# Diagonal key blocks of 384 and 128 queries in one bank with one exponential, and one product for both halves of the rotated sliding keys

## The chip, the core and the metric

The kernel runs on one NeuronCore of a Trainium2 chip. The metric is the device time of one execution in microseconds (us). Engines are named as in the profile: PE is TensorE, DVE is VectorE, ACT is ScalarE, POOL is GpSimd, SP is SyncE, which here issues nearly all DMAs. Each of them takes its instructions in the order in which they were laid down for it, and they meet at semaphores alone. SBUF is the working memory, PSUM the memory that PE writes.

## The reference, cut to what matters

Two transformer blocks are computed one after the other on 2048 tokens of width 1024. The first block has eight heads of "forgetting" attention (called fox in the code) and eight query heads of a sliding-window attention with two key heads. The second has an attention over keys that an indexer selected (called dsa in the code, eight heads, 16 meta tokens ahead of the keys), and beside it a gated recurrence. The lines that the change bears on are these:

```python
half = HEAD_DIM // 2                        # rope, on qb (8 heads) and kb (2 heads)
x1, x2 = xf[..., :half], xf[..., half:]
return concat([x1 * cos - x2 * sin, x2 * cos + x1 * sin], axis=-1)
...
s = einsum('bhqd,bhkd->bhqk', qb, kh) * scale + cb[..., None] - cum[:, :, None, :]
s = where(key_pos <= q_pos, s, -inf)        # causal
p = softmax(s, axis=-1)
return einsum('bhqk,bhkd->bhqd', p, vh)
```

The second attention has the same form, with a mask of selected keys and a bias by distance added to the scores.

## The kernel before

**Number format.** A product of float32 quality is made of three float16 products: each operand is split into a high and a low part, and high x high, high x low and low x high are summed in PSUM.

**The projections of the first block** stream weight blocks through `load_w` (four loads `wraw`, scaled on DVE in L282, cast on ACT in L283, low part on POOL in L284) and multiply each with the normalised activations. `mm3_T` (L319) makes one transposed product: eight steps over the contraction, three products in each (L326, L327, L328), each of 512 columns. `rotated` (L504) makes the queries and keys of the sliding attention. Rope needs the two halves of each head as two separate tensors, so `rotated` makes two products for each of the four groups of 512 tokens, one for each half, in two PSUM tiles `pp` (the pool has two). For the queries each half has 128 rows (four heads of 32), for the keys, the block `kb`, 64 rows (two heads of 32). Four DVE instructions multiply them with cosine and sine (L523 and L524, into tiles `ra`), POOL adds or subtracts (L525), and `store_rot` splits the result (ACT L480, POOL L481, into one of two tiles `ehi`) and writes it to DRAM (L482, `d_kb` for the keys).

**The attention units.** A unit is one head h and one group g of 512 queries. `main` runs over key blocks of 128 keys, j = 0 to 4g + 3. For the last four blocks, those on the diagonal, only the queries from 128 (j - 4g) on count, so they have 512, 384, 256 and 128 columns. In `block`, PE makes the scores in a PSUM tile `pst` (fox L982, L984, the causal mask L986; dsa L2103, L2104, bias L2111 and L2113, key masks L2115), `Att.weights` takes the exponential on ACT (L746), casts it to its high part `phi` (L748 on ACT, a small share in L750 on DVE), subtracts for the low part `plo` (L752, mostly POOL), and `Att.pv` multiplies both with the values, three products for each 128 queries (L776, L777, L778), summed in the PSUM tile `po`. After the last block `norm` divides by the row sums (in dsa after a copy of `po` on ACT, L2123). There are two `pst` tiles in fox and three in dsa, three of each of `p32`, `phi` and `plo`, and one `po`. Beside a unit's blocks runs the preparation of a later one, whose row maxima are found on DVE (L963 in fox, L2058 in dsa) and turned into rows of the query tile (L763 to L769).

**What sets the order.** The program text gives an order and priorities, and a scheduler lays the instructions of each engine down by them and by its own estimate of when each is ready. The order on each engine is therefore a result of the build and can move everywhere when something is changed at one place. The fox units of heads 0 to 3 lie among the projections of the first block, those of heads 4 to 7 among the sliding units and the output projection, the dsa units among the recurrence and the second output projection.

Of the kernel before, what the change touches and what calls it, by code (L numbers as in the profile page):

```python
# [10 lines left out]
F32 = mybir.dt.float32  # L11
# [456 lines left out]
def blocks1(K, A, h, sp, wp, er, ps, pso, fa, cum):  # L468

    nc = K.nc  # L470
# [33 lines left out]
    def rotated(kind, c0, m):  # L504
        def f(w, inv, rn):
# [10 lines left out]
            for g in range(NG):  # L516
                p = [ps.tile([128, 512], F32, name="pp")[:m] for _ in range(2)]
                for a in range(2):
                    mm3_T(K, p[a], w, a * m, h[g])
# [170 lines left out]
def fox_gates(K, A, sp, pp, fa, cum, tag):  # L690
# [28 lines left out]
    nc.vector.tensor_scalar(K.clim, K.clim, 2.0 ** 14, None, op0=ALU.mult)  # L719

# [187 lines left out]
def phase_first(K, A, sk):  # L908
# [4 lines left out]
    with ExitStack() as st, ExitStack() as sr:  # L913
# [59 lines left out]
        def main(g, h, ops):  # L973
            KA, KB, QA, QB, v = ops
            po = pso.tile([128, 4, 65], F32, name="po")

            def block(j):
                s0 = max(0, j - 4 * g)
                c0 = s0 * 128
                ks = slice(j * 128, (j + 1) * 128)  # L980
                p = pst.tile([128, 512], F32, name="pst")
                nc.tensor.matmul(p[:, c0:], lhsT=KA[:69, ks], rhs=QA[:69, c0:], start=True, stop=False)  # L982
                diag = j >= 4 * g
                nc.tensor.matmul(p[:, c0:], lhsT=KB[:, ks], rhs=QB[:, c0:], start=False, stop=not diag)  # L984
                if diag:
                    nc.tensor.matmul(p[:, s0 * 128:s0 * 128 + 128], lhsT=K.idb, rhs=K.mT, start=False, stop=True)  # L986
                hi, lo = at.weights(p[:, c0:], K.fci[:, h // 4:h // 4 + 1])
                for s in range(s0, 4):
                    c = slice((s - s0) * 128, (s - s0) * 128 + 128)
                    at.pv(po[:, s], hi[:, c], lo[:, c], v[:, j], first=j == 0 and s == 0, last=j == 4 * g + s)  # L990
# [987 lines left out]
def phase_dsa(K, A, out):  # L1978

    nc, tc = K.nc, K.tc  # L1980
    with ExitStack() as st:
# [98 lines left out]
        def main(g, h, ops, mk):  # L2080
# [17 lines left out]
            def block(j):  # L2098
                s0 = max(0, j - 4 * g)
                c0 = s0 * 128  # L2100
                ks = slice(16 + j * 128, 16 + (j + 1) * 128)
                p = pst.tile([128, 512], F32, name="pst")
                nc.tensor.matmul(p[:, c0:], lhsT=KA[:66, ks], rhs=QA[:66, c0:], start=True, stop=False)  # L2103
                nc.tensor.matmul(p[:, c0:], lhsT=KB[:, ks], rhs=QB[:, c0:], start=False, stop=False)  # L2104
                if j >= 4 * g - 1:

                    b0 = max(0, min(256, (j - 4 * g) * 128))
                    d0 = 4 * g * 128 + b0 - j * 128
                    for a in range(2):
                        if d0 < 0:  # L2110
                            nc.tensor.matmul(p[:, 384:], lhsT=jr, rhs=bT[:, a, :128], start=False, stop=False)  # L2111
                        else:
                            nc.tensor.matmul(p[:, b0:b0 + 256], lhsT=jr, rhs=bT[:, a, d0:d0 + 256], start=False, stop=False)  # L2113
                for s in range(s0, 4):
                    nc.tensor.matmul(p[:, s * 128:s * 128 + 128], lhsT=mk[s][:, j * 128:(j + 1) * 128], rhs=K.idb, start=False, stop=s == 3)  # L2115
                hi, lo = at.weights(p[:, c0:], K.dci[:, h // 4:h // 4 + 1])
                for s in range(s0, 4):
                    c = slice((s - s0) * 128, (s - s0) * 128 + 128)
                    at.pv(po[:, s], hi[:, c], lo[:, c], v[:, j + 1], last=j == 4 * g + s)
# [214 lines left out]
```

## Time and profile before

| | |
|---|---|
| median of 3 runs | 3169.38 us (3162.87 to 3175.8) |
| the profiled execution: its own time | 3170.48 us |
| its span, first to last instruction | 3168.7 us |
| PE busy | 2822.7 us, 89% |
| DVE, ACT, POOL busy | 2101.6, 1686.9, 1450.2 us |
| matmuls | 25152 |

The span is 1.8 us shorter than the execution's own time, and the execution is 1.1 us over the median. A busy engine here means that some instruction of it is under way. Matmuls overlap each other in the pipeline, so what a matmul takes from PE is read from the distance between the starts of two that follow each other, not from its mean duration.

### The profile page before, as it was taken

To read this page: it belongs to the slowest core of one execution; us is meant where nothing else is said; L and a number is where in the kernel's file an instruction comes from. 1 tells how busy PE (TensorE), PEld (TensorE's weight loads), DVE (VectorE), ACT (ScalarE), POOL (GpSimd) and SP (SyncE) were. 2 spreads that over 40 slices of the span, in tenths; PEclk is the share of its full clock that TensorE was granted. 3 is DMA by queue.
4 is the path that set the end of the run, shared out by engine and by line. 5 is a ranking of instruction groups with operands and counts; after the bars stand their busy time and mean duration, and the time that the engine had idled before them with its cause. 6 is when DMAs were issued, how large, how long until landed. Compare 5 with 4: busy or idle time off the path is not lost. (4 is left out here: it accounts for less than half of the span.)

```text
span 3168.7 us, 65862 instructions
## 1 busy us (share of the span) xinstructions
PE 2822.7 (89%) x25152; PEld 1858.8 (59%) x25152; DVE 2101.6 (66%) x5073; ACT 1686.9 (53%) x3058; POOL 1450.2 (46%) x1241
## 2 busy tenths in 40 slices
PE   7899999999997899999998889899678888988997
PEld 5554444477884555544445665358566566666663
DVE  7523765566678676646499699830578778888763
ACT  4423665576566655634356466321455456657763
POOL 3211446564333555534233433610456567768752
PEclk9899999999996799999999989899679989999998
DMA  6222343532235343334433532222753444443331
GB/s 235 82 87 84 105 129 111 173 95 69 79 94 167 109 142 108 124 91 157 111 97 101 160 125 73 89 91 63 182 159 102 137 133 113 118 117 110 122 97 59
DMA packets 271184, 364.28 MB, mean 115 GB/s; under 512 B 60205, under 2 KB 192033, under 8 KB 269705
## 3 DMA queue, kind: packets, MB, share of 16 engines
q1 hardware_dynamic: 270424, 359.96, 37.8%
q8 instruction: 199, 3.26, 0.4%
q14 instruction: 129, 1.05, 0.1%
q10 hardware_dynamic: 432, 0.02, 0.0%
HBM read 247.05 MB, written 112.82 MB: 114 GB/s over the span
## 5 line engine op out<-in xcount | busy, mean ns | idle before, releaser
L752 POOL TENSOR_TENSOR plo<-p,phi 128x512 f16<-128x512 f32 (+3 forms) x600 | 664.9, 1121 | 569.9 <-ACT phi L748 360.0
L748 ACT CAST phi<-p 128x512 f16<-128x512 f32 (+3 forms) x649 | 347.0, 554 | 84.2 <-PE po L778 75.1
L746 ACT ACTIVATE p<-pst,shift,dci 128x512 f32<-128x512 f32 (+4 forms) x352 | 247.4, 716 | 137.2 <-POOL plo L752 46.7
L778 PE MATMUL po<-v,plo 128*128 128x65 f16 x2176 | 270.1, 196 | 35.0 <-POOL plo L752 27.9
L776 PE MATMUL po<-v,phi 128*128 128x65 f16 x2176 | 286.4, 197 | 5.3 <-ACT phi L748 4.2
L777 PE MATMUL po<-v,phi 128*128 128x64 f16 x2176 | 285.3, 198 | 0.0
L778 PEld LDWEIGHTS <-plo 128*128 128x128 f16 x2424 | 234.7, 101 | 79.2 <-POOL plo L752 46.8
L746 ACT ACTIVATE p<-pst,shift,fci 128x512 f32<-128x512 f32 (+1 forms) x320 | 220.1, 710 | 113.1 <-PE pst L984 70.2
L963 DVE TENSOR_REDUCE mu<-p 128x1 f32<-128x512 f32 (+2 forms) x320 | 188.4, 603 | 130.1 <-PE p L959 83.3
L776 PEld LDWEIGHTS <-phi 128*128 128x128 f16 x2424 | 236.1, 100 | 48.8 <-ACT phi L748 11.4
L284 POOL TENSOR_TENSOR wlo<-wraw,whi 128x512 f16<-128x512 f32 (+3 forms) x116 | 149.9, 1310 | 216.9 <-ACT whi L283 214.0
L2058 DVE CUSTOM_DVE_ANT_0 jk<-p,mk 128x512 bf16<-128x512 f32 (+2 forms) x320 | 193.4, 604 | 80.5 <-PE p L2052 32.8
L777 PEld LDWEIGHTS <-phi 128*128 128x128 f16 x2424 | 235.6, 100 | 15.3 <-issue 1.8
L337 PE MATMUL pp<-whi,hhi 128*128 128x256 f16 (+2 forms) x824 | 235.0, 286 | 7.7 <-ACT whi L283 5.7
L339 PE MATMUL pp<-whi,hlo 128*128 128x256 f16 (+2 forms) x824 | 233.2, 285 | 4.2 <-POOL hlo L465 4.2
L338 PE MATMUL pp<-wlo,hhi 128*128 128x256 f16 (+2 forms) x824 | 234.7, 285 | 0.6 <-POOL wlo L284 0.6
L326 PE MATMUL pp<-hhi,whi 128*128 128x512 f16 (+2 forms) x496 | 190.7, 384 | 4.4 <-DVE ra L523 4.4
L328 PE MATMUL pp<-hhi,wlo 128*128 128x512 f16 (+2 forms) x496 | 190.3, 384 | 0.0
L327 PE MATMUL pp<-hlo,whi 128*128 128x512 f16 (+2 forms) x496 | 190.0, 383 | 0.0
L328 PEld LDWEIGHTS <-wlo 128*128 128x128 f16 (+2 forms) x1000 | 99.7, 100 | 122.6 <-POOL wlo L284 10.9
L326 PEld LDWEIGHTS <-whi 128*128 128x128 f16 (+2 forms) x1000 | 100.5, 101 | 120.1 <-issue 10.2
L327 PEld LDWEIGHTS <-whi 128*128 128x128 f16 (+2 forms) x1000 | 99.9, 101 | 117.3 <-issue 16.0
(666 smaller groups left out, 8933.6 us busy)
## 6 DMA issues: line engine op xcount, KB each, us to landing
wraw<-in_w_in_dram SPq DMA_DIRECT2D x88, 256.0 KB
d_z<-er SPq DMA_DIRECT2D x128, 128.0 KB
bT<-d_rb SPq DMA_DIRECT2D x32, 384.0 KB
wa<-in_w_ada_dram SPq DMA_DIRECT2D x8, 1024.0 KB
x<-in_x_dram SPq DMA_DIRECT2D x16, 512.0 KB
d_k<-ehi SPq DMA_DIRECT2D x32, 256.0 KB
d_q<-ehi SPq DMA_DIRECT2D x32, 256.0 KB
QA<-d_q SPq DMA_DIRECT2D x64, 128.0 KB
```

What stands on the lines that cost most here:

```text
L326: nc.tensor.matmul(ps, lhsT=whi, rhs=hhi[:, kk, :], start=kk == 0, stop=False)
L327: nc.tensor.matmul(ps, lhsT=whi, rhs=hlo[:, kk, :], start=False, stop=False)
L328: nc.tensor.matmul(ps, lhsT=wlo, rhs=hhi[:, kk, :], start=False, stop=kk == KK - 1)
L337: nc.tensor.matmul(ps, lhsT=hhi[:, kk, s], rhs=whi, start=kk == 0, stop=False)
L338: nc.tensor.matmul(ps, lhsT=hhi[:, kk, s], rhs=wlo, start=False, stop=False)
L339: nc.tensor.matmul(ps, lhsT=hlo[:, kk, s], rhs=whi, start=False, stop=kk == KK - 1)
L746: nc.scalar.activation(p, s, AF.Exp, scale=ci[:m], bias=K.shift[:m])
L748: nc.scalar.copy(hi, p)
L752: e.tensor_tensor(lo, p, hi, op=ALU.subtract)
L776: nc.tensor.matmul(o, lhsT=hi, rhs=v[:, :65], start=first, stop=False, **kw)
L777: nc.tensor.matmul(o[:, 1:65], lhsT=hi, rhs=v[:, 65:129], start=False, stop=False, **kw)
L778: nc.tensor.matmul(o, lhsT=lo, rhs=v[:, :65], start=False, stop=last, **kw)
```

## The change

**The keys of the sliding attention.** Where a half has 64 rows (the block `kb` alone), both halves now come from one product of 128 weight columns into one PSUM tile. The first half is its rows 0 to 63. The second, rows 64 to 127, is copied by ACT to rows 0 to 63 of a tile `ra` in SBUF, which the DVE instructions read in the place of the second PSUM tile. This is four groups of 24 products in the place of four of 48, and four copies on ACT more.

**The diagonal.** `key_blocks` lists the blocks of a unit: those up to 4g as before, then 4g + 1 and 4g + 3 together, then 4g + 2. `packed` gives each its place in the bank: block 4g + 1 has 384 columns, block 4g + 3 the 128 behind them. The scores of both are made one after the other in the same PSUM tile, and one exponential, one cast and one subtraction take all 512 columns. The products with the values are the same ones, from other columns of `phi` and `plo`. Both attentions have 32 units, and in each a unit now has one exponential, one cast and one subtraction less. The unit's last block has 256 columns; before it had 128.

```diff
+                if m == 64:
+                    pb = ps.tile([128, 512], F32, name="pp")
+                    mm3_T(K, pb, w, 0, h[g])
+                    z = sp.tile([128, 512], F32, name="ra", tag="ra", bufs=4)[:m]
+                    nc.scalar.copy(z, pb[m:])
+                    p = [pb[:m], z]
+                else:
...
+def key_blocks(g):
+    return [(j,) for j in range(4 * g + 1)] + [(4 * g + 1, 4 * g + 3), (4 * g + 2,)]
+
+def packed(g, js):
+    part, o = [], 0
+    for j in js:
+        s0 = max(0, j - 4 * g)
+        part.append((j, s0, o, 512 - 128 * s0))
+        o += 512 - 128 * s0
+    return part, o
...
-            def block(j):
-                s0 = max(0, j - 4 * g)
...
+            def block(js):
+                p = pst.tile([128, 512], F32, name="pst")
+                part, n = packed(g, js)
+                for j, s0, o, w in part:
+                    ks, c0, x = slice(j * 128, (j + 1) * 128), s0 * 128, p[:, o:o + w]
+                    nc.tensor.matmul(x, lhsT=KA[:69, ks], rhs=QA[:69, c0:], start=True, stop=False, **kw)
...
-                hi, lo = at.weights(p[:, c0:], K.fci[:, h // 4:h // 4 + 1])
+                hi, lo = at.weights(p[:, :n], K.fci[:, h // 4:h // 4 + 1])
...
-            return [lambda j=j: block(j) for j in range(4 * g + 4)] + [norm]
+            return [lambda j=j: block(j) for j in key_blocks(g)] + [norm]
```

Dsa's `block` is changed in the same way. In the part of the program that runs, the order of PE has 96 matmuls less, and that of ACT 127 instructions less, among them four loads of activation tables (16 before, 12 now). The order is laid down anew throughout the two attentions; between them (the projections of the second block and its indexer) it is the same.

**ACT where the sliding keys are made.** Before, from the first store of rotated keys on (`ehi` is the tile that is stored, `wjk` a norm of a weight block that is loaded, `p` and `phi` belong to fox units):

```order
L480 CAST ehi<-ra 64x512
L262 ACTIVATE wjk,wam<-wraw 128x512
L480 CAST ehi<-ra 64x512
L746 ACTIVATE p_3925<-pst,shift,fci 128x256
L748 CAST phi<-p_3884 128x384
L748 CAST phi<-p_3925 128x256
L746 ACTIVATE p_3941<-pst,shift,fci 128x128
L748 CAST phi<-p_3941 128x128
L480 CAST ehi<-ra 64x512 x2
L769 CAST QA<-p_3915 2x512
L746 ACTIVATE p_3970<-pst,shift,fci 128x512
```

Now, from the exponential ahead of the third store on (L774 and L776 are L746 and L748 of before, L522 is the new copy, `whi` the cast of a weight block):

```order
L774 ACTIVATE p_3844<-pst,shift,fci 128x512
L480 CAST ehi<-ra 64x512
L522 COPY ra<-pp 64x512
L774 ACTIVATE p_3882<-pst,shift,fci 128x256
L776 CAST phi<-p_3844 128x512
L776 CAST phi<-p_3882 128x256
L480 CAST ehi<-ra 64x512
L283 CAST whi<-wraw 128x512 x4
L480 CAST ehi<-ra 64x512
L522 COPY ra<-pp 64x512
L262 ACTIVATE wjk,wam<-wraw 128x512 x2
L480 CAST ehi<-ra 64x512
```

The stores stand closer together, the fourth has a weight block's casts right behind it, and the copies of the third and fourth group stand behind stores of the groups before.

**ACT at the end of the last dsa unit.** Before, to the copy of `po` (`pc`) that ends the unit:

```order
L746 ACTIVATE p_43472<-pst,shift,dci 128x512
L748 CAST phi<-p_43445 128x512
L748 CAST phi<-p_43472 128x512
L746 ACTIVATE p_43499<-pst,shift,dci 128x512
L746 ACTIVATE p_43525<-pst,shift,dci 128x384
L748 CAST phi<-p_43499 128x512
L746 ACTIVATE p_43547<-pst,shift,dci 128x256
L748 CAST phi<-p_43525 128x384
L748 CAST phi<-p_43547 128x256
L746 ACTIVATE p_43565<-pst,shift,dci 128x128
L748 CAST phi<-p_43565 128x128
L2123 COPY pc<-po 128x260
```

Now (L2155 is L2123 of before):

```order
L774 ACTIVATE p_42912<-pst,shift,dci 128x512
L776 CAST phi<-p_42912 128x512
L774 ACTIVATE p_42939<-pst,shift,dci 128x512
L774 ACTIVATE p_42966<-pst,shift,dci 128x512
L776 CAST phi<-p_42939 128x512
L776 CAST phi<-p_42966 128x512
L774 ACTIVATE p_42997<-pst,shift,dci 128x512
L774 ACTIVATE p_43022<-pst,shift,dci 128x256
L776 CAST phi<-p_42997 128x512
L776 CAST phi<-p_43022 128x256
L2155 COPY pc<-po 128x260
```

The exponentials of 384 and 128 columns have become one of 512, and the unit's last exponential and cast have 256 columns.

## Rows read from the trace of the kernel before

**Rows 1.** The page of the profile, its head and the first line of part 1: busy time of each engine, share of the span, instructions.

```profile
span 3168.7 us, 65862 instructions
PE 2822.7 (89%) x25152; PEld 1858.8 (59%) x25152; DVE 2101.6 (66%) x5073; ACT 1686.9 (53%) x3058; POOL 1450.2 (46%) x1241
```

**Rows 2.** Busy time by stretches of the span: stretch, its length, then for PE, PEld, DVE, ACT and POOL the busy us and (x) the instructions, then the granted share of the TensorE clock, the DMA share and GB/s. 422 to 490 is where the products of the sliding keys lie, 2200 to 3169 dsa.

```profile
422.00:490.00 68.00, 65.46 (x463) 32.41 (x462) 37.25 (x88) 36.38 (x72) 40.49 (x38) 1.00 0.39 121
2200.00:3169.00 969.00, 815.47 (x9547) 587.91 (x9544) 697.87 (x1468) 549.08 (x913) 580.62 (x454) 0.91 0.43 120
```

**Rows 3.** Groups of PE instructions by line, with shapes kept apart: the first of the three product lines, with weights of 128 rows by 64 columns (sliding keys) and 128 by 128 (the others). The columns are busy us and mean ns of one, then the idle time before them. L327 and L328 have the same counts.

```profile
L326 PE MATMUL pp<-hhi,whi 128*64 128x512 f16 x64 | 24.5, 383 | 1.1 <-DVE ra L523 1.1
L326 PE MATMUL pp<-hhi,whi 128*128 128x512 f16 x424 | 163.1, 385 | 3.3 <-DVE ra L523 3.3
```

**Rows 4.** The timeline of PE inside one product of the sliding keys: start, duration as modelled, instruction.

```profile
443.09 0.38 PE L326 MATMUL pp<-hhi,whi 128*64 128x512 f16 x1
443.31 0.38 PE L327 MATMUL pp<-hlo,whi 128*64 128x512 f16 x1
443.52 0.38 PE L328 MATMUL pp<-hhi,wlo 128*64 128x512 f16 x1
```

**Rows 5.** Groups of ACT instructions by line and shape, columns as in rows 3: the cast of a stored half in SBUF with 64 rows, and the nearest read of a PSUM tile with 64 rows.

```profile
L480 ACT CAST ehi<-ra 64x512 f16<-64x512 f32 x8 | 4.9, 615 | 8.3 <-DMA d_kb<-ehi 8.1 <-POOL ra L525 0.2
L345 ACT ACTIVATE ehi<-pp,ik 64x512 f16<-64x512 f32 x4 | 2.7, 678 | 6.8 <-PE pp L328 4.5 <-PE spo L778 2.3
```

**Rows 6.** Timeline of ACT and of SP where the sliding keys are stored; in brackets the idle time before and what ended it. Of the two rows of SP each stands for the issue of two stores.

```profile
460.14 0.62 ACT L480 CAST ehi<-ra 64x512 f16<-64x512 f32 x1 [4.61 <-DMA d_kb<-ehi]
464.21 0.62 ACT L480 CAST ehi<-ra 64x512 f16<-64x512 f32 x1 [3.46 <-DMA d_kb<-ehi]
...
454.65 1.18 SPq L482 DMA_DIRECT2D d_kb<-ehi  x2
462.43 4.16 SPq L482 DMA_DIRECT2D d_kb<-ehi  x2
```

**Rows 7.** Groups of ACT instructions by line and shape, columns as in rows 3: exponentials and casts of the attention blocks.

```profile
L746 ACT ACTIVATE p<-pst,shift,dci 128x512 f32<-128x512 f32 x224 | 171.1, 775 | 72.5 <-POOL plo L752 36.3 <-PE pst L2115 19.2 <-POOL wmlo L752 5.0
L746 ACT ACTIVATE p<-pst,shift,dci 128x384 f32<-128x384 f32 x32 | 21.4, 669 | 15.3 <-PE pst L2115 8.6 <-POOL plo L752 3.5 <-DVE plo L752 3.0
L746 ACT ACTIVATE p<-pst,shift,dci 128x256 f32<-128x256 f32 x32 | 18.0, 563 | 11.1 <-POOL plo L752 4.4 <-POOL wmlo L752 2.8 <-PE pst L2115 2.6
L746 ACT ACTIVATE p<-pst,shift,dci 128x128 f32<-128x128 f32 x32 | 14.6, 455 | 4.4 <-POOL plo L752 2.5 <-PE pst L2115 1.6
L748 ACT CAST phi<-p 128x512 f16<-128x512 f32 x462 | 276.5, 615 | 47.0 <-PE po L778 41.2 <-PE po L777 1.1 <-PE spo L778 0.6
L748 ACT CAST phi<-p 128x384 f16<-128x384 f32 x64 | 32.5, 510 | 13.7 <-PE po L778 13.3
L748 ACT CAST phi<-p 128x256 f16<-128x256 f32 x60 | 24.1, 401 | 2.7 <-PE po L778 2.3
L748 ACT CAST phi<-p 128x128 f16<-128x128 f32 x63 | 18.7, 297 | 20.7 <-PE po L778 18.2 <-PE po L777 2.1
```

**Rows 8.** The same view for POOL: the low parts.

```profile
L752 POOL TENSOR_TENSOR plo<-p,phi 128x512 f16<-128x512 f32 x421 | 528.5, 1266 | 411.4 <-ACT phi L748 264.6 <-issue 22.7 <-PE po L778 17.3
L752 POOL TENSOR_TENSOR plo<-p,phi 128x384 f16<-128x384 f32 x65 | 65.6, 1012 | 79.0 <-ACT phi L748 48.3 <-PE p L962 12.7 <-PE po L777 5.9
L752 POOL TENSOR_TENSOR plo<-p,phi 128x256 f16<-128x256 f32 x54 | 44.0, 814 | 28.3 <-ACT phi L748 15.2 <-PE p L959 4.8 <-PE po L778 3.0
L752 POOL TENSOR_TENSOR plo<-p,phi 128x128 f16<-128x128 f32 x60 | 29.5, 491 | 51.1 <-ACT phi L748 31.8 <-PE wsum L239 5.1 <-PE p L959 3.1
```

**Rows 9.** Waits of PE from 430 to 1450 us, by waiting line and releaser: us in total, times, longest.

```profile
PE po L778 <- POOL plo L752: 6.8, 11, 1.7
PE pst L982 <- ACT p L746: 6.1, 10, 1.6
PE pp L326 <- DVE ra L523: 4.4, 3, 2.9
PE po L776 <- ACT phi L748: 3.9, 3, 3.0
PE po L778 <- DVE plo L752: 1.5, 2, 1.3
```

**Rows 10.** The same view from 2200 to 3169 us.

```profile
PE p L768 <- DVE zrow L765: 31.3, 11, 8.4
...
PE po L778 <- POOL plo L752: 19.7, 25, 3.3
PE po L778 <- DVE plo L752: 3.0, 2, 1.8
PE pst L2103 <- ACT p L746: 1.2, 5, 0.3
```

**Rows 11.** Timeline of ACT at the end of the last dsa unit, with idle time before and releaser in brackets.

```profile
3111.29 0.56 ACT L746 ACTIVATE p<-pst,shift,dci 128x256 f32<-128x256 f32 x1
3113.88 0.82 ACT L748 CAST phi<-p 128x384 f16<-128x384 f32 x2 [2.02 <-PE po L778]
3115.07 0.46 ACT L746 ACTIVATE p<-pst,shift,dci 128x128 f32<-128x128 f32 x1 [0.37 <-PE pst L2115]
...
3117.28 0.38 ACT L2123 COPY pc<-po 128x260 f32<-128x260 f32 x1 [1.43 <-PE po L778]
```

More of the change, by code (lines that the diff above doesn't have):

```diff
@@ L516, in f @@
             for g in range(NG):
-                p = [ps.tile([128, 512], F32, name="pp")[:m] for _ in range(2)]
-                for a in range(2):
-                    mm3_T(K, p[a], w, a * m, h[g])
+                if m == 64:
[5 more added lines that the diff above has]
+                else:
+                    p = [ps.tile([128, 512], F32, name="pp")[:m] for _ in range(2)]
+                    for a in range(2):
+                        mm3_T(K, p[a], w, a * m, h[g])
                 tb = [table(g, a)[:m] for a in range(2)]
@@ L2096, in meta, with block @@
                     at.pv(po[:, s], hi[:, c], lo[:, c], v[:, 0], first=s == 0)
[L2098 to L2101, printed above, removed]
+            def block(js):
                 p = pst.tile([128, 512], F32, name="pst")
[L2103 to L2119, printed above, removed]
@@ new lines, in block @@
+                part, n = packed(g, js)
+                kw = dict(skip_group_check=len(js) > 1)
+                for j, s0, o, w in part:
+                    ks, c0, x = slice(16 + j * 128, 16 + (j + 1) * 128), s0 * 128, p[:, o:o + w]
+                    nc.tensor.matmul(x, lhsT=KA[:66, ks], rhs=QA[:66, c0:], start=True, stop=False, **kw)
+                    nc.tensor.matmul(x, lhsT=KB[:, ks], rhs=QB[:, c0:], start=False, stop=False, **kw)
+                    if j >= 4 * g - 1:
+                        b0 = max(0, min(256, (j - 4 * g) * 128))
+                        d0 = 4 * g * 128 + b0 - j * 128
+                        for a in range(2):
+                            if d0 < 0:
+                                nc.tensor.matmul(x, lhsT=jr, rhs=bT[:, a, :128], start=False, stop=False, **kw)
+                            else:
+                                nc.tensor.matmul(x[:, b0 - c0:b0 - c0 + 256], lhsT=jr, rhs=bT[:, a, d0:d0 + 256], start=False, stop=False, **kw)
+                    for s in range(s0, 4):
+                        nc.tensor.matmul(x[:, (s - s0) * 128:(s - s0) * 128 + 128], lhsT=mk[s][:, j * 128:(j + 1) * 128], rhs=K.idb, start=False, stop=s == 3, **kw)
@@ L2121, in norm @@
+                hi, lo = at.weights(p[:, :n], K.dci[:, h // 4:h // 4 + 1])
+                for j, s0, o, _ in part:
+                    for s in range(s0, 4):
+                        c = slice(o + (s - s0) * 128, o + (s - s0) * 128 + 128)
+                        at.pv(po[:, s], hi[:, c], lo[:, c], v[:, j + 1], last=is_last(g, j, s))
             def norm():
@@ L2124, in norm @@
                 at.norm(pc, K.vinv[:, h:h + 1], h, o_rows(K.d_a, D, g, h // 2 * 128), key="on")
-            return [meta] + [lambda j=j: block(j) for j in range(4 * g + 4)] + [norm]
+            return [meta] + [lambda j=j: block(j) for j in key_blocks(g)] + [norm]
         def close_hg():
```

21 lines of the change are left out of this document (11 added, 10 removed).

## The prediction

> **What bounds the kernel now.** I read the head of the page first: PE has work under way for 89% of the span, DVE for 66%, ACT for 53%, POOL for 46% [rows 1]. PE is the bound on the whole, but an average doesn't tell what one stage is worth, so I went to the two places that the change touches. First the stretch in which the sliding keys are projected, 422 to 490 us: PE is busy for 65.46 of 68 us at a granted clock of 1.00, the upper of its two levels, while DVE, ACT and POOL have 36 to 41 us of work [rows 2]. Here PE's own work sets the time. Then the two attentions. From 2200 us on (dsa) PE is busy for 815 of 969 us [rows 2], so I read the waits: which of PE's idle time ends with an exponential, a cast or a low part? In the fox stretch these are 6.8 + 6.1 + 3.9 + 1.5 = 18.3 us [rows 9], in dsa 19.7 + 3.0 + 1.2 = 23.9 us [rows 10], together 42.2 us. The largest single wait in dsa, 31.3 us, is for the row maxima of a later unit, which come from DVE [rows 10]; the change leaves that work alone.
>
> **The sliding keys, PE.** Before, 64 products on each of three lines, 192 in all, have a 64-column weight [rows 3]; half of them go. Their starts are 443.09, 443.31 and 443.52, which is (443.52 - 443.09) / 2 = 0.215 us apart [rows 4]. The weight that is twice as wide costs nothing: the group with 128 weight columns has a mean of 385 ns against 383 [rows 3]. So 96 x 0.215 = 20.6 us of PE's work goes from a stretch where PE is the bound.
>
> **The sliding keys, the rest.** The four copies lie between two rows: 0.615 us (a cast of 64 rows inside SBUF) and 0.678 us (a read of 64 rows from PSUM) [rows 5]. They read PSUM, so I take 0.68, in sum 2.7 us of ACT. ACT has 36.38 us of work in these 68 us [rows 2], so the cover is its own idle time. A new wait comes with each copy, though: it stands in ACT's queue for a product, and behind it stand exponentials and casts of fox units, for which PE's value products wait; and two of the four DVE instructions now wait for the copy too. One wait should go: PE stood 4.4 us for DVE to give back a `pp` tile [rows 9]; a group now takes one of the two tiles and not both.
>
> What is late next in the shorter stretch? If all of the 20.6 us came off, 68 would become 47.4 us, with POOL at 40.5 and ACT at 36.4 + 2.7 = 39.1 us of it [rows 2]: tight, but room. Tighter are the stores. There are two `ehi` tiles for eight stores. In the trace ACT stood 4.61 and 3.46 us in front of the third and the fourth cast until earlier stores had landed [rows 6], 8.1 us in all [rows 5]. A store issued at 454.65 freed its tile at 460.14, 5.5 us later, and SP issues stores behind other loads in its queue [rows 6]. Then PE had products to chew on, of which half are gone now. If all six casts after the first two wait for about 4 us each, ACT needs 39.1 + 24 = 63 us, and the stretch shrinks by only 5 us. The gain therefore lies between 5 and 20.6 us. In the new order the fourth cast has the weights for the next product block right behind it, while the rest of the key products, a gate block and fox products stand on PE in the meantime, about as much as the round of a store takes. I take 15 us, nearer to the upper end, because PE didn't stall in front of the two waits that are in the trace.
>
> **The diagonal.** Per unit one exponential, cast and low part of 384 and of 128 columns become those of 512 columns. Exponential: 0.669 + 0.455 - 0.775 = 0.349 us; cast: 0.510 + 0.297 - 0.615 = 0.192 us [rows 7]; low part: 1.012 + 0.491 - 1.266 = 0.237 us [rows 8]. For 64 units that is 34.6 us of ACT and 15.2 us of POOL. PE's work is the same to the column. Neither ACT nor POOL is full, so this is not time by itself: it counts where PE waits for the chain, in the 42.2 us above. Both ends: nothing, if these waits come from chains with other timing, and all of the 42.2 us. One in ten chains of this kind disappears (64 of 320 fox and 320 dsa), worth some 4 us; and where four blocks passed through `pst`, `p32`, `phi` and `plo`, three do, so that a tile comes free earlier for the next block, which I count at as much again. I take 8 us, range -5 to 21.
>
> The order of a unit's end changes as well. Its last block has 256 columns in the place of 128, so the last chain is longer by (0.563 + 0.401 + 0.814) - (0.455 + 0.297 + 0.491) = 0.535 us [rows 7, 8]. Against that, ACT has less ahead of it: exponentials and casts of 384, 256 and 128 columns take 2.895 us, those of 512 and 256 take 2.354 us, 0.541 us less [rows 7]. I cost the two together at nothing. At the end of the last unit ACT stood 2.02 us for PE to give back a `phi` tile and 0.37 us for scores, and 6 us passed from the 256-column exponential to the copy of `po` [rows 11]; with one block less, a microsecond or two should go there, and this is part of the 8 us.
>
> The four table loads that ACT no longer makes and the new order of the rest (the trace of before shows neither) I cost at zero, within plus or minus 10 us.
>
> **Sum.** The profiled execution took 3170.5 us, its span 3168.7 [rows 1]; the median of the runs is 1.1 us lower. 3170.5 - 15 - 8 = 3147.5; against the median 3169.4 - 23 = 3146 us, 0.7% less.
>
> **Rivals.** *The stores hold the keys' stretch.* ACT waits for `ehi` tiles in front of nearly every cast, the stretch loses 5 us in the place of 15, and the attention's waits move to other rows and stay as long: 3169.4 - 5 - 4 = 3160 us. For it: two of the six casts that could wait did [rows 6], and the cover shrinks. Against it: a PE that was busy for 96% of the stretch all the same [rows 2].
>
> *Coarser instructions make PE wait more (slower).* The place is the end of each unit. The packed exponential can't start until the scores of both blocks are there, and the last chain is 0.535 us longer. Where ACT is not the one that is late, its shorter queue gives nothing back, and 64 x 0.535 = 34 us come on top: 3169.4 - 15 + 34 = 3188 us. It decides when PE has no other products between the scores of the last block and its value products. For it: PE does wait for `plo`, 25 times in dsa [rows 10]. Against it: the longest of these waits is 3.3 us and they fall on 25 places among 32 units of up to 17 blocks, and at the end of the last unit ACT stood for PE, not PE for ACT [rows 11]. The Trainium skill has this as a rule (Perfetto Trace Analysis, Optimizing Scalar/DVE Operations): where ScalarE isn't saturated but causes bubbles on other engines, breaking instructions up may let work finish sooner, and grouping pays when the engine is saturated. By that rule, with ACT at 53%, this rival would be the likely one.
>
> *Both gains come in full*, or nearly: 20.6 us from the keys and half of the 42.2 us of waits: 3169.4 - 42 = 3128 us.
>
> That the change doesn't do what it says is excluded for the diagonal, since the exponentials of 384 and 128 columns are gone from the new order; for the keys it is the first rival.
>
> **How the numbers follow.** The forecast, 3130 to 3153 us, has a chance of 0.50; both gains in full, under 3130, 0.14; the first rival, up to 3168, 0.27; a new order that loses the gain again, 3168 to 3185, 0.03; slower 0.06. The range reaches from 3169.4 - 20.6 - 21 - 10 = 3118 up to 3168, where the keys give 5 us and the diagonal costs 4; it leaves out some 0.15. What this kernel's measurement can tell from no change is about 0.5%, 15.8 us, so faster means below 3153.5: 0.64; within it 0.30; slower 0.06.
>
> **What would show it.** In the profile after: 25056 matmuls; PE's stretch of the sliding keys shorter by 15 to 20 us, still over 90% busy; ACT's waits for `d_kb` not over some 10 us (24 would be the first rival); ACT busy for 30 to 38 us less, POOL for some 15; the waits of PE for `plo`, `phi` and `p` in the two attentions about 8 us shorter. If they are longer, and longest at the ends of units, the second rival holds. A time within the range that comes from PE's waits for the row maxima, or for loads, would make the sum right by luck.

## The result and the profile after

The changed kernel took 3191.31 us in the median of 6 runs (3183.64 to 3199.22), the kernel before 3166.15 us in 6 runs beside it (3154.7 to 3175.8): a ratio of 1.0079, 95% interval 1.0052 to 1.0106. So it is slower by 0.8%, some 25 us; 3146 was predicted, 3168 was the upper end, and slower had a chance of 0.06. The profiled execution took 3184.65 us, 14.2 us more than the one before; it is among the shortest of the six, so the pair of profiles shows only part of the 25 us.

The head of the page after, against [rows 1]:

```profile
span 3182.9 us, 65375 instructions
PE 2808.6 (88%) x25056; PEld 1849.8 (58%) x25056; DVE 2097.6 (66%) x5068; ACT 1664.1 (52%) x2931; POOL 1427.7 (45%) x1181
```

The work that was to go is gone: 96 matmuls, 22.8 us of ACT (30 to 38 predicted), 22.5 us of POOL (15 predicted). On ACT the durations of all instructions sum to 37.1 us less; but the records of neighbours overlap, and a merged instruction takes its overlap with it, so the busy time falls by less than a sum of mean durations says. The span is longer all the same, so engines wait more. Busy time by stretches (columns as in [rows 2]), the sliding keys and dsa:

```profile
422.00:490.00 68.00, 52.26 (x345) 26.28 (x344) 46.74 (x96) 33.07 (x66) 44.69 (x38) 0.90 0.44 135
2200.00:3182.00 982.00, 819.74 (x9530) 586.59 (x9527) 696.51 (x1468) 538.37 (x848) 568.62 (x422) 0.90 0.42 119
```

In the keys' stretch PE was busy for 65.46 of 68 us at a granted clock of 1.00 [rows 2]. Now it is 52.26 us at 0.90, and no engine is near full: DVE, the next, has 46.74 us. What PE waited for there, from 430 to 500 us (us in total, times, longest):

```profile
PE p L987 <- DVE mu L991: 5.0, 2, 4.3
PE wsum L239 <- DVE wa L237: 4.1, 1, 4.1
PE pp L326 <- DVE ra L532: 3.7, 3, 3.0
PE p L796 <- DVE zrow L793: 1.1, 1, 1.1
PE pp L635 <- DVE ra L532: 0.9, 1, 0.9
PE pst L1011 <- ACT QA L797: 0.4, 1, 0.4
```

These are 15.2 us, where before only these two stood:

```profile
PE p L768 <- DVE zrow L765: 1.4, 1, 1.4
PE pp L326 <- DVE ra L523: 1.1, 1, 1.1
```

That is 12.7 us of waits more; and a clock of 0.90 over 70 us is up to another 7 us. The two are up to 20 us, and 20.6 us of products had been taken away. One of the three longest waits, followed back in the timeline (start, duration, instruction, and in brackets the idle time before it and its releaser):

```profile
481.22 0.59 PE L239 MATMUL wsum<-wa,ones 128*128 128x1 f32 x2 [4.13 <-DVE wa L237]
...
480.02 0.41 DVE L642 TENSOR_TENSOR er<-er 1x256 f32<-1x256 f32 x1 [6.44 <-DMA er<-in_g_post_dram]
481.03 0.14 DVE L237 TENSOR_REDUCE wa<-wam 128x1 f32<-128x4 f32 x1
...
467.42 0.63 SPq L372 DMA_DIRECT2D sK<-d_kb  x1
473.66 0.47 SPq L641 DMA_DIRECT2D er<-in_g_post_dram  x1
```

PE wants `wa` for the next weights; `wa` stands in DVE's queue behind L642, which waits for a load of 256 numbers (`er`); SP issued that load at 473.66 us, behind the loads of `sK`. And those had waited on SP for the keys' stores:

```profile
SPq L372 <- DMA d_kb<-ehi: 5.9, 1, 5.9
```

The other two of the three stand behind DVE instructions that are themselves slow:

```profile
458.09 4.54 DVE L282 TENSOR_SCALAR wraw<-wraw,ws 128x512 f32<-128x512 f32 x4
462.75 0.67 DVE L991 TENSOR_REDUCE mu<-p 128x1 f32<-128x512 f32 x1
463.48 0.59 PE L987 MATMUL p<-KA,QA 69*128 69x512 f16 x1 [4.34 <-DVE mu L991]
...
457.45 1.59 POOL L481 TENSOR_TENSOR ehi<-ra,ehi 64x512 f16<-64x512 f32 x1
459.01 1.44 POOL L533 TENSOR_TENSOR ra<-ra 64x512 f32<-64x512 f32 x1
460.42 1.15 POOL L284 TENSOR_TENSOR wlo<-wraw,whi 128x512 f16<-128x512 f32 x1
...
436.64 3.51 DVE L778 CAST phi<-p 128x512 f16<-128x512 f32 x1
440.08 0.73 DVE L532 SCALAR_TENSOR_TENSOR ra<-pp,inv,cs 64x512 f32<-64x512 f32 x1
440.87 0.39 PE L326 MATMUL pp<-hhi,whi 128*128 128x512 f16 x1 [3.03 <-DVE ra L532]
```

Four scalings (L282) took 4.54 us, where the four from 431.75 us on took 1.65, and the last two of them, after POOL had stopped, only 0.87; one cast (L778) took 3.51 us, where the 47 of its size take 0.71 in the mean. Beside both, POOL worked without a gap (457.45 to 461.57, and from 435.94 to past the end of the cast).

Before, with 20 us more of products, 2.5 us of waits showed in the same stretch. ACT's own waits for `d_kb` are 6.0 us in three places, against 8.1 [rows 5].

Up to the start of dsa the two profiled executions then stand level: the last `out1` product starts at 1465.7 us before and at 1462.6 after, the first score product of dsa's blocks at 2236.7 and 2235.8. In these two executions the 14 us are lost in dsa, 932.0 us before and 947.0 after. PE's waits there, to be read beside [rows 10]:

```profile
PE p L796 <- DVE zrow L793: 31.0, 11, 9.7
PE po L806 <- POOL plo L780: 23.8, 31, 2.2
...
PE y L1175 <- DVE oTlo L346: 14.9, 6, 4.6
...
PE po L806 <- DVE plo L780: 3.4, 4, 1.1
...
PE pst L2134 <- ACT p L774: 0.2, 1, 0.2
```

and from 430 to 1450 us, beside [rows 9]:

```profile
PE po L806 <- POOL plo L780: 9.0, 14, 1.5
...
PE po L804 <- ACT phi L776: 6.2, 5, 2.6
...
PE po L806 <- DVE plo L780: 3.0, 5, 1.6
...
PE pst L1011 <- ACT p L774: 1.8, 6, 0.5
```

The lines that made up my 42.2 us come to 20.0 us in fox (18.3) and 27.4 in dsa (23.9): 5 us more, not 8 less. The largest new wait is none of them. The output projection's second product waits for `oTlo` for 14.9 us, in code that the change doesn't touch; before it was:

```profile
PE y L1145 <- DVE oTlo L346: 3.8, 2, 2.7
```

At its longest, 4.64 us, `oTlo` stood in DVE's queue behind other work that fills dsa:

```profile
2413.11 1.17 DVE L1877 TENSOR_TENSOR dc<-dc 128x64 f32<-128x64 f32 x1
2414.21 2.19 DVE L1980 TENSOR_TENSOR o<-o,rs 128x1024 f32<-128x1024 f32 x1
2416.32 0.68 DVE L2088 CUSTOM_DVE_ANT_0 jk<-p,mk 128x512 bf16<-128x512 f32 x1
2416.93 0.08 DVE L2088 DVE_READ_ACCUMULATOR2_ANT mu<- 128x1 f32 x1
2416.93 1.80 DVE L1877 TENSOR_TENSOR dc<-dc 128x32 f32<-128x32 f32 x1
2418.66 0.74 DVE L346 SCALAR_TENSOR_TENSOR oTlo<-y,as__91,oThi 128x512 f16<-128x512 f32 x1
...
2419.45 0.59 PE L1175 MATMUL y<-wohi,oThi 128*128 128x512 f16 x1 [4.64 <-DVE oTlo L346]
```

That is the order which the scheduler laid, not a cost of an instruction that the change adds. So two questions went to the chip: where the keys' 20.6 us went, and what a new order costs by itself.

### The profile page after: what moved, and what is told of

The parts are those of the page before. It is cut to its first block, busy times and chain, and to the rows that moved or that the text cites. A ratio compares the mean times of both kernels' runs of the same rounds, so it can differ in the third digit from the quotient of the medians.

```text
span 3182.9 us, 65375 instructions
## 1 busy us (share of the span) xinstructions
PE 2808.6 (88%) x25056; PEld 1849.8 (58%) x25056; DVE 2097.6 (66%) x5068; ACT 1664.1 (52%) x2931; POOL 1427.7 (45%) x1181
## 5 line engine op out<-in xcount | busy, mean ns | idle before, releaser
L780 POOL TENSOR_TENSOR plo<-p,phi 128x512 f16<-128x512 f32 (+2 forms) x539 | 636.5, 1193 | 536.6 <-ACT phi L776 356.6
L776 ACT CAST phi<-p 128x512 f16<-128x512 f32 (+1 forms) x586 | 338.0, 593 | 67.0 <-PE po L806 43.3
L774 ACT ACTIVATE p<-pst,shift,dci 128x512 f32<-128x512 f32 (+1 forms) x320 | 236.4, 753 | 140.0 <-PE pst L2146 51.5
L806 PE MATMUL po<-v,plo 128*128 128x65 f16 x2176 | 263.4, 195 | 40.9 <-POOL plo L780 33.7
L774 ACT ACTIVATE p<-pst,shift,fci 128x512 f32<-128x512 f32 (+1 forms) x288 | 210.0, 751 | 96.7 <-PE pst L1013 54.6
L326 PE MATMUL pp<-hhi,whi 128*128 128x512 f16 (+1 forms) x464 | 177.5, 383 | 5.1 <-DVE ra L532 3.7
L327 PE MATMUL pp<-hlo,whi 128*128 128x512 f16 (+1 forms) x464 | 177.8, 383 | 0.0
L328 PE MATMUL pp<-hhi,wlo 128*128 128x512 f16 (+1 forms) x464 | 177.3, 383 | 0.0
L326 PEld LDWEIGHTS <-whi 128*128 128x128 f16 (+1 forms) x968 | 96.4, 100 | 120.7 <-ACT whi L283 9.6
L328 PEld LDWEIGHTS <-wlo 128*128 128x128 f16 (+1 forms) x968 | 95.9, 100 | 118.9 <-POOL wlo L284 10.7
L327 PEld LDWEIGHTS <-whi 128*128 128x128 f16 (+1 forms) x968 | 95.8, 100 | 108.5 <-issue 10.7
## 6 DMA issues: line engine op xcount, KB each, us to landing
wa<-in_w_ada_dram SPq DMA_DIRECT2D x8, 1024.0 KB
x<-in_x_dram SPq DMA_DIRECT2D x16, 512.0 KB
```

The lines of the kernel that those rows point to most:

```text
L326: nc.tensor.matmul(ps, lhsT=whi, rhs=hhi[:, kk, :], start=kk == 0, stop=False)
L327: nc.tensor.matmul(ps, lhsT=whi, rhs=hlo[:, kk, :], start=False, stop=False)
L328: nc.tensor.matmul(ps, lhsT=wlo, rhs=hhi[:, kk, :], start=False, stop=kk == KK - 1)
L774: nc.scalar.activation(p, s, AF.Exp, scale=ci[:m], bias=K.shift[:m])
L776: nc.scalar.copy(hi, p)
L780: e.tensor_tensor(lo, p, hi, op=ALU.subtract)
```

## The experiments

Ratios are to the kernel before, run beside it, with the 95% interval.

**The parts alone.** keys_alone is the first piece of the diff on the kernel before; fox_alone and dsa_alone are its pieces in one attention, with the helpers:

```diff
-            return [lambda j=j: block(j) for j in range(4 * g + 4)] + [norm]
+            return [lambda j=j: block(j) for j in key_blocks(g)] + [norm]
...
-            return [meta] + [lambda j=j: block(j) for j in range(4 * g + 4)] + [norm]
+            return [meta] + [lambda j=j: block(j) for j in key_blocks(g)] + [norm]
```

order_alone only exchanges the last two blocks of a unit, in both attentions (the marks of the last product, which follow suit, are left out here):

```diff
-            return [lambda j=j: block(j) for j in range(4 * g + 4)] + [norm]
+            return [lambda j=j: block(j) for j in [*range(4 * g + 2), 4 * g + 3, 4 * g + 2]] + [norm]
```

Keys alone: 

> The kernel before with the product of the sliding keys alone; the blocks of both attentions as before. PE has 20.6 us less work. My prediction's term for this part: 15 us less, 3151. Theory now (the stretch runs dry: with half the products PE has nothing left while ACT, SP and the stores go round once per group): the first 1464 us get 0 to 5 us shorter, PE is busy for under 85% of 440 to 490 us. Rival (the single product saves what it should, and the packing in fox loses it again): the first 1464 us get 15 to 20 us shorter. The order of dsa is laid anew here although nothing of it is edited: whatever dsa's length changes by, against 969 us from 2200 us on, is the size of what a new order does by itself; I expect under 5 us either way.

Fox alone: 

> The kernel before with the packed blocks in fox alone. My prediction's term: some 4 us less. Theory now (the packing gives nothing, since PE's waits for phi and plo come at the ends of units as before): the first 1464 us within 5 us of before. Rival (packed chains make PE wait more at unit ends): 32 units by 0.5 us, 17 us longer, and PE's waits for phi, plo and p in 430 to 1450 us, 18.3 us before, at 30 or more. dsa has a new order here too, with no edit in it: under 5 us either way expected.

Dsa alone: 

> The kernel before with the packed blocks in dsa alone; all engines have the order of before up to the first packed block, so the first 2200 us are those of before within 2 us. My prediction's term: some 4 us less from there on. Theory now (what after loses, it loses in dsa, by the packing itself): 12 to 20 us more, near 3182. Rival (it is the order that the scheduler lays and not the packing): within 8 us of before, on either side.

Order alone: 

> The kernel before with the last two key blocks of each unit exchanged (the one of 128 queries ahead of the one of 256), in both attentions, nothing packed: the same instructions, the last chain of a unit longer by 0.535 us, no instruction taken from ACT or POOL. By the rival of the longer unit end: 64 by 0.535 is 34 us more, 3200; half of it where PE has other work, 3183. By the theory that the end of a unit is covered: within 8 us of before.

Measured: keys alone 1.0028 (1.0013 to 1.0043), fox alone 1.0006 (0.9991 to 1.0020), dsa alone 0.9994 (0.9976 to 1.0011), order alone 1.0013 (0.9997 to 1.0029). Neither packing shows a gain or a loss, nor does a longer unit end. The single product, the part that I had priced highest, is slower, by less than a new order alone turns out to cost below. For dsa alone the theory misses, since the packing does not cost 12 to 20 us there, and its rival holds, within 8 us of before. For keys alone the last `out1` product comes at 1479.0 us, 13 us later than before, where the theory had it 0 to 5 us earlier and the rival 15 to 20. From 430 to 500 us, first dsa alone (up to 2200 us the order of before), then keys alone:

```profile
430.00:500.00 70.00, 68.85 (x520) 35.54 (x517) 40.69 (x88) 36.59 (x74) 47.04 (x44) 1.00 0.39 115
```

```profile
430.00:500.00 70.00, 53.46 (x369) 27.59 (x368) 46.22 (x96) 36.93 (x77) 46.51 (x41) 0.85 0.38 116
```

In keys alone the longest wait of PE, 7.08 us, stood behind one DVE instruction that took 5.06 us; before, each of its kind took 0.73 to 0.74. The timeline:

```profile
470.11 5.06 DVE L531 SCALAR_TENSOR_TENSOR ra<-ra,inv,cs 64x512 f32<-64x512 f32 x1 [2.48 <-POOL ehi L481]
475.10 1.11 DVE L773 SCALAR_TENSOR_TENSOR zrow<-zrow,t 128x4 f16<-128x4 f16 x1
...
470.04 3.36 POOL L284 TENSOR_TENSOR wlo<-wraw,whi 128x512 f16<-128x512 f32 x3
473.37 1.25 POOL L533 TENSOR_TENSOR ra<-ra 64x512 f32<-64x512 f32 x1
474.59 1.59 POOL L284 TENSOR_TENSOR wlo<-wraw,whi 128x512 f16<-128x512 f32 x1
...
476.27 0.64 PE L776 MATMUL p<-idh,zrow 128*66 128x128 f16 x4 [7.08 <-DVE zrow L773]
```

L531 reads the copied half, which is in SBUF, where it read PSUM before. It seemed the culprit, so the copy was taken apart next.

**The copy, and the parts together.** keys_no_copy and after_no_copy read the upper half from PSUM; copy_alone keeps both products of before and copies; diag_both packs in both attentions and leaves the keys as before. The first edit is shown against the changed kernel, the second (copy_alone) against the kernel before.

```diff
-                    z = sp.tile([128, 512], F32, name="ra", tag="ra", bufs=4)[:m]
-                    nc.scalar.copy(z, pb[m:])
-                    p = [pb[:m], z]
+                    p = [pb[:m], pb[m:]]
```

```diff
                     mm3_T(K, p[a], w, a * m, h[g])
+                if m == 64:
+                    z = sp.tile([128, 512], F32, name="ra", tag="ra", bufs=4)[:m]
+                    nc.scalar.copy(z, p[1])
+                    p[1] = z
```

Keys without the copy: 

> The kernel before with the single product of the sliding keys, but no copy: VectorE reads the second rotated half straight from PSUM (rows 64 to 127) and writes rows 0 to 63. Theory now (a VectorE instruction that multiplies the copied half reads SBUF alone and stands while GpSimd works: 0.73 us from PSUM, up to 5.06 us in the keys-alone trace, with zrow behind it and PE 7.1 us behind that): all 16 take 0.73 to 0.74 us again, the stretch 430 to 500 us wins 8 to 15 us of PE's waits back, and the run takes 8 to 15 us less than with the copy, 0.995 to 1.000 of before. Rival (the stretch runs dry because half the products are gone, whoever reads them): still 1.002 to 1.004.

Copy alone: 

> The kernel before with both products of the sliding keys, but the second rotated half copied to SBUF by ScalarE and read from there, as after the change. Theory now (the read from SBUF costs): 5 to 12 us longer than before, 1.002 to 1.004, with the 8 VectorE instructions on the copied half at more than 0.9 us in the mean. Rival (the halved products cost, not the copy): 0.999 to 1.001.

Both packings: 

> The changed kernel with the sliding keys as before: the packed blocks in both attentions. Packed in fox alone came out at 1.0006 and in dsa alone at 0.9994 of before. If the parts add up: 1.000, within 0.002 either way. Rival (a packed fox hands dsa an order that costs): over 1.003. My prediction's term was 8 us less, 0.9975.

After without the copy: 

> The changed kernel without the copy, the second half read from PSUM: everything that the change does, and VectorE's reads as before. If the copy is the cost and the packing is worth nothing: as the single product without the copy, 0.995 to 1.000 of before. By my prediction's sum it would be 0.993. Rival (the change loses by its new order in both attentions, wherever the keys are read from): 1.005 to 1.008, as the changed kernel.

Measured: 1.0028 (1.0010 to 1.0047), 1.0078 (1.0047 to 1.0109), 1.0047 (1.0031 to 1.0063) and 1.0066 (1.0046 to 1.0087). My theory of the copy fell: without it all 16 instructions take 0.73 to 0.75 us again, and the time is the same. PE is still dry, now on other waits:

```profile
430.00:500.00 70.00, 52.69 (x348) 26.36 (x344) 43.53 (x91) 32.35 (x72) 42.42 (x39) 0.88 0.37 110
```

In copy_alone the 8 reads from SBUF take 0.955 us in the mean, 1.8 us more in sum, and PE is busy for 66.79 of the 70 us; yet it loses 25 us, more than either of its theories had. And the packings, 1.0006 and 0.9994 apart, are 1.0047 together. Costs of instructions don't do that; orders might.

**Neutral orders.** The attention deals out casts and low parts by running totals of columns. Starting them elsewhere changes which block's cast or low part goes to which engine, and through that the order of all engines in both attentions; in the traces of the three shifts of before the number of casts and of low parts on each engine changes by at most two, of 736 each. Shift 1, on the kernel before and on the changed one (shift 2: 2560.0 and 1536.0, shift 3: 1024.0 and 512.0):

```diff
-        self.done = {"hi": [0.0, 0.0], "lo": [0.0, 0.0]}
+        self.done = {"hi": [1536.0, 0.0], "lo": [1024.0, 0.0]}
```

Before, shift 1: 

> The kernel before with nothing of the change: only the running totals by which the attention deals out casts and low parts start at 1536 and 1024 columns of ScalarE's and GpSimd's share instead of 0. The work is the same (some ten low parts go from VectorE to GpSimd); which block's cast and low part goes where is shifted, and with it the order of all engines in both attentions. Theory now (a new order by itself costs: the order of before is a good draw, and what the change loses is that draw): 1.002 to 1.007 of before. Rival (orders are worth the same, the cost is the change's own instructions): 0.999 to 1.001.

Before, shift 2: 

> As the first shift of the kernel before, with the totals at 2560 and 1536 columns (one low part goes from VectorE to GpSimd): a second new order of the same work. Theory now (a new order costs): 1.002 to 1.007 of before, and the two shifts differ by some 0.002. Rival (orders are worth the same): 0.999 to 1.001.

Before, shift 3: 

> The kernel before with nothing of the change, the running totals of the dealing starting at 1024 and 512 columns: a third new order of the same work. The two others were 1.0075 and 1.0057. If the order of before is a good draw among many: 1.001 to 1.008. If the first two were bad luck: about 1.000.

After, shift 1: 

> The changed kernel with the first shift of the totals. Theory now (a new order is a new draw, and the change itself is worth little): between 0.999 and 1.008 of before, so not at 1.0079 again; the mean over the changed kernel and its two shifts lies within 0.003 of the mean of before's two shifts. Rival (the change's own instructions cost): 1.006 to 1.010, whatever the order.

After, shift 2: 

> The changed kernel with the second shift of the totals. As for the first: theory now 0.999 to 1.008 of before, and other than the first shift by some 0.002; rival 1.006 to 1.010. By my prediction's sum, if the shift took nothing away, 0.993.

After, shift 3: 

> The changed kernel with the third shift. The changed kernel was 1.0079, its shifts 1.0007 and 1.0027. If the change is worth nothing in the mean, and orders spread: anywhere in 0.999 to 1.008. If the packing and the single product are worth my prediction's 23 us and the draw takes it away: the mean of the changed kernel's four orders lies 0.007 under the mean of the three shifts of before.

Measured: before 1.0075 (1.0048 to 1.0103), 1.0057 (1.0038 to 1.0076), 1.0035 (1.0019 to 1.0052); after 1.0007 (0.9988 to 1.0026), 1.0027 (1.0010 to 1.0043), 1.0047 (1.0030 to 1.0064). Nothing of the change is in the first three, and they are slower than before by 0.56% in the mean, 18 us: the order of before is a good one. order_alone is a fourth order of the same instructions, longer unit end included, at 1.0013; with it the mean is 1.0045, 14 us, and a new order by itself costs anything from 4 to 24 us here. With its own 1.0079 the changed kernel has a mean of 1.0040 over four orders, 0.0016 under the three shifts of before, with a standard error of 0.0019 from the spread of the two groups. So in the mean over orders the changed kernel is 5 us shorter, give or take some 12 (two standard errors). With order_alone among those of before it is 2 us, give or take 13, and with the three shifts alone on both sides 9, give or take 10. The 23 us of my sum lie outside each time, but with so few orders not by much.

**PE's work in the stretch.** short_products and short_keys leave out two of the three terms of the sliding products, for keys and queries or for keys alone (`kind == "kb"`); keys_twice computes the keys' products a second time.

```diff
+        if short:
+            continue
         nc.tensor.matmul(ps, lhsT=whi, rhs=hlo[:, kk, :], start=False, stop=False)
...
-                    mm3_T(K, p[a], w, a * m, h[g])
+                    mm3_T(K, p[a], w, a * m, h[g], short=kind in ("kb", "qb"))
```

```diff
                     mm3_T(K, p[a], w, a * m, h[g])
+                    if kind == "kb":
+                        mm3_T(K, p[a], w, a * m, h[g])
```

Short products: 

> The kernel before with two of the three terms left out of the sliding keys' and queries' products (128 and 256 matmuls of 512 columns at 0.215 us: 82.6 us of PE's work); everything else as before. Theory now (in fox PE's work is the pace only over a longer stretch; a saving returns once it is larger than what the next waits take): 40 to 70 us less than before, 0.978 to 0.987. Rival A (fox is paced by something else than PE, which is why the 20.6 us came back as waits): 0 to 20 us less. Rival B (a saving counts in full, apart from the draw of the order, which is 0.001 to 0.0075): 83 us less plus 3 to 24, 0.975 to 0.981.

Keys twice: 

> The kernel before with the sliding keys' products computed twice over: 192 more matmuls of 512 columns at 0.215 us, 41.3 us more of PE's work, in the same stretch. If PE's work sets the time there in both directions, with a mean draw of the order: 41 plus 3 to 24 us more, 1.014 to 1.020. If the stretch had waits to fill: under 25 us more, 1.008 or less.

Short keys: 

> The kernel before with two of the three terms left out of the sliding keys' products alone: 128 matmuls of 512 columns at 0.215 us, 27.5 us less of PE's work in the stretch where the change takes 20.6, with no copy, no packing, and both halves from two products. Theory now (430 to 500 us has no other work for PE there, whichever way the products go): PE is busy for under 57 of 70 us between 430 and 500 us at a granted clock under 0.95, as in all seven kernels with the single product and in none of the nine without, and the last out1 product stays where it was, within the draw of the order (1472 us, 8 either way). Rival (it is the copy, the shared tiles or the packing): over 63 of 70 us busy at 1.00, the last out1 product near 1472 - 27 = 1445 us.

Measured: 0.9908 (0.9889 to 0.9927), which is 29 us less for 82.6 us of PE's work; 1.0147 (1.0127 to 1.0167), 47 us more for 41.3 us; 1.0006 (0.9986 to 1.0026), nothing for 27.5 us. The first lies between its theories, the second inside the dearer one. Short keys decides: no copy, no packing, two products, and PE dries up as it did in the changed kernel:

```profile
430.00:500.00 70.00, 55.58 (x434) 28.38 (x432) 51.47 (x105) 37.80 (x77) 46.49 (x44) 0.86 0.42 127
```

Its longest waits there are for yet others (4.5 us for `p` from ACT, 3.9 for `mu`). The table has, from each profiled execution, PE's busy time from 430 to 500 us with the granted clock, the start of the last `out1` product, and the length of dsa from its first block's scores to the end of the span. Each row is a single execution, and not all ran on the same chip. A yardstick is the stage between the two marks, from the last `out1` product to dsa's first scores: PE has the same 4419 matmuls there in every kernel, and it takes 764 to 779 us. Two rows that differ by less than some 15 us are not told apart.

| kernel | PE of 70 us | clock | last out1, us | dsa, us |
|---|---|---|---|---|
| before | 67.51 | 1.00 | 1465.7 | 932.0 |
| dsa_alone | 68.85 | 1.00 | 1463.5 | 931.5 |
| fox_alone | 68.20 | 1.00 | 1471.8 | 926.6 |
| order_alone | 68.21 | 1.00 | 1469.5 | 927.7 |
| before_shift1 | 67.96 | 1.00 | 1485.0 | 949.1 |
| before_shift2 | 66.95 | 1.00 | 1463.4 | 946.8 |
| before_shift3 | 66.90 | 0.98 | 1464.7 | 940.5 |
| copy_alone | 66.79 | 1.00 | 1479.6 | 941.9 |
| diag_both | 68.18 | 1.00 | 1480.1 | 940.2 |
| keys_twice | 67.76 | 1.00 | 1502.4 | 941.8 |
| after | 54.62 | 0.90 | 1462.6 | 947.0 |
| keys_alone | 53.46 | 0.85 | 1479.0 | 935.6 |
| keys_no_copy | 52.69 | 0.88 | 1487.4 | 932.7 |
| after_no_copy | 43.97 | 0.78 | 1473.5 | 941.1 |
| after_shift1 | 53.70 | 0.85 | 1457.4 | 937.2 |
| after_shift2 | 53.61 | 0.88 | 1473.3 | 941.1 |
| after_shift3 | 53.72 | 0.84 | 1470.3 | 942.1 |
| fox_shift1 | 53.68 | 0.88 | 1464.5 | 966.6 |
| short_keys | 55.58 | 0.86 | 1466.2 | 935.9 |
| short_products | 52.11 | 0.88 | 1450.1 | 927.1 |

The nine kernels with all of the products and nothing doubled reach the last `out1` product at 1471.5 us in the mean (1463.4 to 1485.0), the eight with the single product at 1471.0 (1457.4 to 1487.4), with a standard error of the difference of 4.3 us: the 20.6 us are not there.

**A try at a faster one.** fox_shift1 is the changed kernel with shift 1 in fox alone and dsa's blocks as before:

```diff
         at = Att(K, pp, sm, ps1, 0.85, 0.8)
+        at.done = {"hi": [1536.0, 0.0], "lo": [1024.0, 0.0]}
```

> The changed kernel's first shift (1.0007) with the blocks of dsa as before and its totals from 0: all engines have the first shift's order up to dsa, whose last out1 product came 6 to 8 us earlier than with the order of before. If that order repeats its time: the last out1 product at 1455 to 1460 us. dsa is laid anew, 927 to 949 us so far: 0.996 to 1.003 of before, and the only try here at a kernel that is faster than both.

Measured: 1.0096 (1.0067 to 1.0125), a miss. Up to dsa the order is that of after_shift1, and the last `out1` product came at 1464.5 us in the place of 1457.4: one order repeats itself within some 7 us. dsa took 966.6 us, with the very instructions that take 932.0 in the kernel before. No version that computes everything is faster than the kernel before beyond the error.

## Why the prediction was wrong

**The sliding keys: the step that failed.** I took 15 us, between 5 and 20.6, "because PE didn't stall in front of the two waits that are in the trace". The runs give 0.5 us at the last `out1` product, with a standard error of 4.3: my 15 and my upper bound are not there, and only the lower one, 5 us, is not excluded. The work went, 20.6 us of it, but PE's waits and a lower clock in the same 70 us took its place: 44 to 55 us busy in each of the eight kernels with the single product, and the same in short_keys, which loses the products in another way. I had asked what else is late and looked at ACT's waits for `ehi` alone; ACT waits 6.0 us there, less than before. Of the changed kernel's three longest waits one, 4.1 us, stood behind SP's queue (`sK` behind the keys' stores, small loads behind `sK`, DVE behind a load, PE behind DVE), and two, 4.3 and 3.0 us, behind DVE instructions that took three and five times as long as others of their kind while POOL worked, as in keys_alone; in short_keys the longest was for ACT. PE at 96% and 1.00 said that PE's work was the pace, not that nothing stood just under it. My first rival had the stores and a shorter gain, but by ACT and not by SP. Which chain would be next if one of these were taken away stays open; no run shows one single chain behind all of them. Above the pace of the others PE's work does count: keys_twice costs 47 us for 41.3, a new order included, and its last `out1` product comes 31 us after the mean of the nine.

**The new order, costed at zero within 10 us either way.** This is the term that makes the sign. The scheduler lays the order of both attentions anew after each of these edits; three shifts without any other change cost 11 to 24 us, 18 in the mean, and order_alone 4. The same instructions of dsa, packed in none of them, take 926.6 to 966.6 us in the kernels above. With 0 for the keys, 0 for the packing and 18 for the order the sum would have been 3187, against 3191 measured; that the two are so close says little, since single orders lie 20 us apart. My range had the 10 us of the order at its lower end and not at its upper one; with them it would have reached 3178, still short. My "new order that loses the gain again" had a chance of 0.03.

**The diagonal, -8 us.** Not seen, and too small to be excluded. Seven kernels with packed blocks in dsa take 940.0 us there in the mean, the twelve without (and without the exchange) 939.7, with a standard error of the difference of 3.7 us. In fox the last `out1` product of the eight packed ones comes at 1469.2 us in the mean, of ten unpacked ones (short_products and keys_twice left out) at 1472.4, with a standard error of 3.9. So neither shows a gain, and the 4 us that I had for each attention could hide in both. ACT and POOL did get 23 us less to do each: as I wrote, neither is full. PE's waits for the chain grew by 5 us.

**The second rival** gave 3188, and that is where the time came out, but not by its mechanism. order_alone has the longer unit end without any saving, and is at 1.0013 where 34 us would be 1.0107; packed in fox alone and in dsa alone are at 1.0006 and 0.9994. So the rule that I named there (the Trainium skill, Perfetto Trace Analysis, Optimizing Scalar/DVE Operations) is not what decided: coarser instructions on an unsaturated ScalarE cost nothing that these runs can tell, and gained nothing either.

## What to carry to other kernels

Before pricing work that leaves a full engine, look at what that engine does in the same stretch once the work is gone: leave some of it out in a kernel that need not compute anything useful, and see whether the end moves. Where a scheduler lays the order, a change of under one per cent can't be judged from one order: shift something neutral in both kernels and compare the means, since a kernel whose order happens to be a good one loses by many an edit, whatever the edit is worth.

## What the runs showed of the hardware

A VectorE instruction with both of its large operands in SBUF can stand while GpSimd works: 5.06 us for one that takes 0.73 to 0.74 from PSUM, through three low parts and an addition of GpSimd that followed each other without a gap (the timeline of keys_alone); GpSimd's next one then took 1.59 us in the place of some 1.15. The trace of after_shift2 has the same once more, 5.06 us beside three low parts and an addition. The Trainium skill has this (SBUF — State Buffer, Who interferes with whom: a DVE instruction with two SBUF inputs contends with a GpSimd instruction that reads SBUF), and the trace agrees. I had priced the copy and not what reading the copy does. In the changed kernel a cast and a scaling, which read one tensor each, stood beside a busy GpSimd too: 3.51 us in the place of 0.71, and 4.54 us for four scalings in the place of 1.65.

The clock follows the waits. With all products the granted clock is 1.00 from 430 to 500 us (0.98 in one kernel of ten); in the ten kernels with fewer products, in which PE stood for several us at a time there, it falls to 0.78 to 0.90, part of the stretch at the lower of the two levels (1.2 GHz). In the changed kernel it is 0.50 from 462.9 to 469.7 and from 480.0 to 486.8 us, and each time it falls late in one of PE's two waits of over 4 us. So a stretch that dries up pays a second time: in the changed kernel 12.7 us more of waits and up to 7 us of clock.
